# Moving the first half's depthwise convolution wholly to DVE, with the taps split over two running sums

## The chip, the cores and the metric

The kernel runs on one core of one Trainium2 chip. The metric is the device time of one execution in microseconds (us). The engines are named as the profile names them: PE multiplies matrices, DVE is the vector engine, ACT the scalar engine, POOL the small general engine, and SP issues the transfers (DMAs).

## The reference

A two-layer causal trunk over 2048 positions and 1024 channels, in float32. Layer 0 mixes a causal pooling branch with a state-space branch. Layer 1, which the change touches, is a convolution module; `h` is the RMS-normalised input.

```python
proj = einsum('bsd,de->bse', h, w_in)              # 1024 -> 3072
val, gt, z = proj[..., :1024], proj[..., 1024:2048], proj[..., 2048:]
g = val * sigmoid(gt)
# depthwise causal convolution, width 31, one kernel per channel
c = conv(g, conv_w, padding=[(30, 0)]) + conv_b
c = (c - mean(c)) * rsqrt(var(c) + 1e-5) * ln_g + ln_b   # over the channels
y = silu(c) * silu(z)
x = x + einsum('bse,ed->bsd', y, w_out)
```

A final RMS norm follows.

## The kernel before

**Tiles.** The sequence is cut into two halves of 1024 positions, A (h = 0) and B (h = 1), and the channels of layer 1 into eight tiles j = 0 to 7 of 128. Activations lie with channels on the partitions. Every large projection is done in three products, high by high, high by low and low by high parts of the two factors, so a 128-channel output tile over 1024 positions (a unit, such as `A.v3` for the value tile 3 of half A) is 48 matmuls of 512 columns on PE. A unit's sums lie in one of three PSUM buffers `mm`; two smaller PSUM buffers `aux` serve everything else.

**Order on PE.** Layer 0 of A and of B come first, then: A's layer-0 output (`A.glu*`, `A.o.*`), A's layer-1 units (`A.g0` gate, `A.v0` value, and so on, then `A.y0` to `A.y7` for z), B's layer-0 output, B's layer-1 units, A's last projection `A.q.*`, B's last projection `B.q.*`. The table `ORDER` gives the order of the gate and value tiles within a half.

**The convolution.** `post_val` forms the tile g and stores it. Most tiles are convolved on DVE: `conv_load` brings the tile and its 30 positions of history into a buffer `cg`, ACT writes the first tap with the bias into an accumulator `ca`, and `conv_thread` runs the other 30 taps, each `ca = cg[shifted] * weight + ca`, on DVE at the lowest priority. There are two `cg` and two `ca` buffers, so one tile is loaded while the other is summed. The last two tiles of B are done in two passes of 512 positions. The tiles listed in `PEC` are convolved on PE in half B, and those in `PEB` in both halves at once: `pe_conv` builds banded matrices on ACT (24 products of a band with a mask per half tile) and multiplies them in 48 matmuls a tile, whose moving operand has `M = 64 * len(halves)` columns. Before the change DVE has tiles 0 to 5 of A and 0 to 3 of B, and PE has tiles 6 and 7 of both halves together (M = 128) and tiles 4 and 5 of B (M = 64).

**Layer norm.** `ln_thread(h, b)` waits for all eight convolved tiles of a block of 512 positions (b = 0 or 1), loads them into four buffers, and works on DVE and ACT, with three small groups of PE products (mean, variance, spread of the rate) and POOL for the reciprocal root. A's result goes to DRAM (`y1d`) and is loaded again by `y1_thread` when `A.q` is near; B's stays in SBUF.

**What sets the order.** A planner in the kernel (`Sched`) runs at build time. Each piece of work is a thread that yields operations with an assumed duration; the planner picks the operation that can start first, and among those that can start almost as early the one of best priority. The result is one fixed queue for each engine. On the chip each engine runs its queue strictly in that order, and waits where an operand is not there. So a change of the table, of an assumed cost or of the number of buffers moves rows in every queue.

Of the kernel before, what the change touches and what calls it, by code (L numbers as in the profile page):

```python
# [14 lines left out]
AF = mybir.ActivationFunctionType  # L15
ALU = mybir.AluOpType
# [4 lines left out]
H = 1024  # L21
NK = D // 128
# [3 lines left out]
NT = 31  # L26
# [12 lines left out]
SLOTS = dict(act=25, w=8, raw=2, st=8, po=2)  # L39
NSSM = 3  # L40
RANK = dict(split=2, pool=4, pec=3, lna=8, lnb=3, y1=3, ssm=4, prep=2)
PEB = (6, 7)
PEC = (4, 5) + PEB
ORDER = (range(NK), (0, 1, 6, 7, 2, 3, 4, 5))


VECS = {"even_norm": 8, "odd_norm": 8, "pool_scale": 4, "ssm_d": 4, "conv_b": 8, "conv_ln_g": 8, "conv_ln_b": 8}
# [29 lines left out]
class Sched:  # L77
# [24 lines left out]
    def free(self, pool, *tiles):  # L102
        for t in tiles:
            self.pools[pool].append(self.slot.pop(t.tensor.name))

    def done(self, *key):
        self.keys.add(key)

    def spawn(self, gen, prio, name=""):
        self.threads.append(Thread(gen, prio, name))  # L110
# [137 lines left out]
def trunk(ctx, tc, io):  # L248
    nc = tc.nc
    V, A, G, SP = nc.vector, nc.scalar, nc.gpsimd, nc.sync  # L250
    sc = Sched()
    done, free, spawn = sc.done, sc.free, sc.spawn
# [9 lines left out]
    def slots(pool, n, width=1024, where=const):  # L262
        sc.pool(pool, n, lambda i, dt, name: where.tile([128, width], dt, tag=f"{pool}{i}", name=name))
# [4 lines left out]
    slots("st", SLOTS["st"], SLOT)  # L268
    slots("po", SLOTS["po"], SLOT)
    slots("cg", 2, SLOT)  # L270
    slots("ca", 2)
    slots("sml", 12, 16)
    slots("pwt", 1, 128)
    slots("sml2", 1, 64)
# [17 lines left out]
    def width(o):  # L292
        return int(np.prod(o.shape[1:]))
# [20 lines left out]
    def tt(o, a, b, op, eng=None):  # L314
        if eng is G:
            d = 0.35 + 0.2 * width(o) if op == ALU.pow else 0.19 + width(o) * 2e-3
            return Op("G", d, [a, b], [o], lambda: G.tensor_tensor(o, a, b, op))  # L317
        d = vdur(0.16, 1.035e-3, o, a, b)
        return Op("V", d, [a, b], [o], lambda: V.tensor_tensor(o, a, b, op))  # L319
# [14 lines left out]
    def stt(o, a, s, b, op0, op1):  # L334
        rd = [a, b] + ([s] if isinstance(s, bass.AP) else [])
        d = vdur(0.27, 0.935e-3, o, a, b) if isps(a, b) else vdur(0.2, 1.06e-3, o, a, b)
        return Op("V", d, rd, [o], lambda: V.scalar_tensor_tensor(o, a, s, b, op0, op1))  # L337
# [18 lines left out]
    def act(o, a, fn, **kw):  # L356
        rd = [a] + [s for s in kw.values() if isinstance(s, bass.AP)]
        wr = [o]
        if "accum_out" in kw:
            rd.remove(kw["accum_out"])  # L360
            wr.append(kw["accum_out"])
        n = sum(isinstance(s, bass.AP) for s in kw.values())
        return Op("A", adur(o, a, n), rd, wr, lambda: A.activation(o, a, fn, **kw))  # L363
# [24 lines left out]
    def mmb(batch):  # L388

        d = 0.0  # L390
        for o, w, x, s, e in batch:
            if x.dtype == F32R:
                d += width(o) / 2216.0
            elif w.shape[1] > 64:
                d += max(0.224, width(o) * 1e-3)
            else:
                d += 0.07 + width(o) * 0.5e-3

        def emit():
            for o, w, x, s, e in batch:  # L400
                nc.tensor.matmul(o, w, x, start=s, stop=e)  # L401
        rd = []
        wr = []
        for o, w, x, s, e in batch:
            for l, ap in ((rd, w), (rd, x), (wr, o)):
                if not any(ap is y for y in l):
                    l.append(ap)
        op = Op("PE", d, rd, wr, emit)
        op.n = len(batch)
        return op  # L410
# [24 lines left out]
    cwt = ctile("cwt", (128, NK, NT))  # L435
# [16 lines left out]
    def vc(nm, k):  # L452
        return vcol[:, cols[nm] + k:cols[nm] + k + 1]
# [974 lines left out]
    def conv_load():  # L1428
        for h, j in conv_order:
            yield Wait(("g", h, j))  # L1430
            gt = yield Alloc("cg")
            if h == 0:
                yield gset(gt[:, :HL], 0.0)
            else:
                yield dma(gt[:, :HL], gd[0][j][:, H - HL:H])
            yield dma(gt[:, HL:HL + H], gd[h][j])
            cgt[h, j] = gt
            yield Wait(("cw",))
            ca = cas[h, j] = yield Alloc("ca")
            yield act(ca[:, :H], gt[:, 0:H], AF.Identity, bias=vc("conv_b", j), scale=cwt[:, j, 0:1])  # L1440
            done("cg", h, j)

    cgt, cas = {}, {}

    def conv_thread():

        seq = [(h, j, (0, 1)) for h, j in conv_order[:-2]]
        seq += [(h, j, (b,)) for b in range(2) for h, j in conv_order[-2:]]
        for h, j, bl in seq:
            yield Wait(("cg", h, j))  # L1450
            gt, ca = cgt[h, j], cas[h, j]
            n0, n1 = bl[0] * 512, bl[-1] * 512 + 512
            acc = ca[:, n0:n1]
            for k in range(1, NT):
                yield stt(acc, gt[:, k + n0:k + n1], cwt[:, j, k:k + 1], acc, ALU.mult, ALU.add)
            if bl[-1] == 1:
                free("cg", gt)
            spawn(conv_store(h, j, ca, bl), 6, f"cs{h}{j}")

    def conv_store(h, j, ca, bl):  # L1460
        n0, n1 = bl[0] * 512, bl[-1] * 512 + 512
        yield dma(cd[h][j // 2][:, j % 2, n0:n1], ca[:, n0:n1])
        if bl[-1] == 1:
            free("ca", ca)
        for b in bl:
            done("c", h, j, b)
# [15 lines left out]
    def pe_conv(n, j):  # L1482


        halves = (0, 1) if j in PEB else (1,)
        M = 64 * len(halves)
# [51 lines left out]
    def post_val(h, j):  # L1538
        def f(ps):
            yield Wait(("th", h, j))  # L1540
            th = th1.pop((h, j))
            t = th[:, :H]
            if j in PEB or (h == 1 and j in PEC):
                n = PEC.index(j)
# [40 lines left out]
    def ln_thread(h, b, out, gate=None):  # L1585
        if gate:
            yield Wait(gate)
        bs = slice(b * 512, (b + 1) * 512)
        for j in range(NK):
            yield Wait(("c", h, j, b))  # L1590
        if h == 0 or b == 0:
            ct = yield Alloc("act", 4)
            pools = ("act",) * 4
        else:
            pools = ("ca", "ca", "cg", "cg")
            ct = yield Alloc("ca", 2)
            ct += yield Alloc("cg", 2)
        cc = [c[:, :1024] for c in ct]
        for kp in range(4):
            yield dma(k2(cc[kp]), cd[h][kp][:, :, bs])  # L1600
        sm_, vs_, q_ = yield Alloc("st", 3)
        sm, vs, sq = sm_[:, :1024], vs_[:, :1024], q_[:, :1024]
        yield tt(sm, cc[0], cc[1], ALU.add)
        for c in cc[2:]:
            yield tt(sm, sm, c, ALU.add)
        yield tt(sm[:, 0:512], sm[:, 0:512], sm[:, 512:1024], ALU.add)
        mups = yield Alloc("aux")
        yield mmb([(mups, onesN, sm[:, 0:512], True, True)])
        mub = mups.rearrange("p (o t) -> p o t", o=1).to_broadcast([128, 2, 512])
        for kp in range(4):  # L1610
            yield tt(k2(cc[kp]), k2(cc[kp]), mub, ALU.subtract)
        free("aux", mups)
        yield act(vs, cc[0], AF.Square)
        for kp in range(1, 4):
            s = sq if kp % 2 else sm
            yield act(s, cc[kp], AF.Square)
            yield tt(vs, vs, s, ALU.add)
        yield tt(vs[:, 0:512], vs[:, 0:512], vs[:, 512:1024], ALU.add)
        var = yield Alloc("aux")
        yield mmb([(var[:, t:t + 1], vs[:, t * 128:(t + 1) * 128], onesN[:, 0:1], True, True) for t in range(4)])  # L1620
        s = yield Alloc("sml")
        va, rs = s[:, 0:4], s[:, 4:8]
        yield ts(va, var[:, :4], LN_EPS, None, ALU.add)
        free("aux", var)
        yield from rsqrt_of(rs, va, 4)
        dg = sm[:, 0:512]
        for t in range(4):
            yield ts(dg[:, t * 128:(t + 1) * 128], ident, rs[:, t:t + 1])
        rps = yield Alloc("aux")
        yield mmb([(rps[:, t * 128:(t + 1) * 128], ones1, dg[:, t * 128:(t + 1) * 128], True, True) for t in range(4)])  # L1630
        free("sml", s)
        rsb = vs[:, 0:512]
        yield acopy(rsb, rps)
        free("aux", rps)
        free("st", q_, sm_)
        rb = rsb.rearrange("p (o t) -> p o t", o=1).to_broadcast([128, 2, 512])
        for kp in range(4):
            yield tt(k2(cc[kp]), k2(cc[kp]), rb, ALU.mult)
            spawn(ln_out(h, b, kp, cc[kp], out, pools[kp], ct[kp]), 2, f"ln{h}{b}{kp}")
        free("st", vs_)  # L1640
# [102 lines left out]
    y1 = [Acts(f"y1{p}") for p in P]  # L1743
# [107 lines left out]
    spawn(after(("y1d", 0, 3), ln_thread(0, 1, None)), RANK["lna"], "lnA1")  # L1851
    spawn(y1_thread(0, y1[0], ("u", GATE_Y)), RANK["y1"], "y1A0")
    spawn(after((y1[0].name, 7, 0), y1_thread(1, y1[0], ("u", GATE_Y))), RANK["y1"], "y1A1")
    spawn(ln_thread(1, 0, y1[1]), RANK["lnb"], "lnB0")
    spawn(ln_thread(1, 1, y1[1]), RANK["lnb"], "lnB1")
    spawn(fnb_thread(0, ("u", "A.q.e0t3")), 4, "fnb")
    done("fnb", 1)
    sc.run()
# [42 lines left out]
```

## Time and profile before

| | |
|---|---|
| median of 3 runs | 1502.55 us (1501.55 to 1502.56) |
| the profiled execution's own time | 1500.32 us |
| its span, first to last instruction | 1498.5 us, so 1.82 us lie around it |
| PE busy | 98% |
| DVE busy | 74% |
| ACT busy | 35% |
| POOL busy | 6% |
| granted PE clock, mean | 0.995 |
| DMA | 276 MB, 184 GB/s |

The profiled execution is 2.23 us below the median. Sums are made against the profiled execution, and the result is carried over to the median. Times in the text are us from the start of the span. A row of the timeline has the start, the length, the engine, the line of the code, the operation, what it writes and reads, and how many instructions were merged; in square brackets stands the time that the engine sat idle just before it and what ended that.

### The profile page before, as it was taken

The numbers are of one execution on the slowest core, as the hardware profiler recorded it, in microseconds if no ns is written. First come the engines' busy times: TensorE is split into PE (matmuls) and PEld (weight loads), VectorE is DVE, ScalarE is ACT, GpSimd is POOL, SyncE is SP. The second block draws the span as 40 slices with busy tenths as digits, with TensorE's granted clock in tenths as the row PEclk, the third lists the DMA queues.
The fourth block names the chain that finished last, engine by engine and source line by source line (L and its number), as shares of the span: only waits on it lengthen the run. The fifth ranks groups of instructions, "written<-read, shape, count | busy, mean of one in ns | idle before, by whom it ended". The sixth has DMA issues, their size and how long they took to land. (4 is left out here: it accounts for less than half of the span.)

```text
span 1498.5 us, 17919 instructions
## 1 busy us (share of the span) xinstructions
PE 1467.7 (98%) x6768; PEld 1202.1 (80%) x6768; DVE 1104.4 (74%) x1333; ACT 524.7 (35%) x834; POOL 89.7 (6%) x297
## 2 busy tenths in 40 slices
PE   7999899999999999999999999999999999999997
PEld 5887688888888888888888888888888788887785
DVE  7988583997975224699999998247987998987632
ACT  6235341112143035211111521352364556544411
POOL 1000100000000011000000000110000000003321
PEclk9999999999999999999999999999999999999999
DMA  9579946556475462331343543524557475957752
GB/s 350 197 212 335 336 165 247 194 189 239 161 268 151 125 206 85 112 111 59 99 127 113 210 140 128 183 70 128 109 156 227 138 244 185 385 202 248 260 171 109
DMA packets 161159, 276.26 MB, mean 184 GB/s; under 512 B 53184, under 2 KB 83632, under 8 KB 161072
## 3 DMA queue, kind: packets, MB, share of 16 engines
q1 hardware_dynamic: 161072, 275.12, 55.5%
q8 instruction: 53, 0.87, 0.2%
q14 instruction: 34, 0.28, 0.1%
HBM read 181.56 MB, written 93.51 MB: 184 GB/s over the span
## 5 line engine op out<-in xcount | busy, mean ns | idle before, releaser
L401 PE MATMUL mm<-act,w 128*128 128x512 f32 x4224 | 1003.8, 397 | 9.6 <-ACT act L363 6.6
L401 PEld LDWEIGHTS mm<-act,w 128*128 128x128 f32 x4224 | 793.2, 189 | 190.5 <-ACT act L363 6.6
L337 DVE SCALAR_TENSOR_TENSOR ca<-cg,cwt,ca 128x1024 f32<-128x1024 f32 (+1 forms) x360 | 397.5, 1106 | 12.8 <-ACT ca L363 2.5
L401 PE MATMUL mm<-w,act 128*128 128x512 f32 x1344 | 315.9, 395 | 0.8 <-DVE w L319 0.8
L401 PEld LDWEIGHTS mm<-w,act 128*128 128x128 f32 x1344 | 251.7, 188 | 59.4 <-DVE w L319 1.1
L319 DVE TENSOR_TENSOR w<-raw,w 128x1024 fp32r<-128x1024 f32 (+1 forms) x119 | 141.9, 1195 | 106.8 <-ACT w L351 106.1
L351 ACT CAST w<-raw 128x1024 fp32r<-128x1024 f32 (+1 forms) x119 | 121.6, 1022 | 214.9 <-PE mm L401 141.6
L363 ACT ACTIVATE junk<-st 128x1024 bf16<-128x1024 f32 (+1 forms) x64 | 54.0, 844 | 123.8 <-DVE st L319 116.1
L319 DVE TENSOR_TENSOR st<-st,mm 128x512 f32<-128x512 f32 x48 | 30.9, 683 | 76.2 <-PE mm L401 76.2
L351 ACT CAST act<-st 128x512 fp32r<-128x512 f32 (+1 forms) x64 | 51.8, 855 | 57.2 <-DVE st L337 16.6
L363 ACT ACTIVATE po<-mm 128x1024 f32<-128x1024 f32 x28 | 28.7, 1025 | 112.4 <-PE mm L401 70.7
L319 DVE TENSOR_TENSOR act<-st,act 128x512 fp32r<-128x512 f32 (+1 forms) x64 | 56.4, 922 | 14.7 <-ACT act L351 14.6
L401 PE MATMUL aux<-st,act 128*128 128x128 f32 (+2 forms) x448 | 63.8, 289 | 0.0
L363 ACT ACTIVATE act<-act,mask 128x128 f32<-128x128 f32 x192 | 58.0, 392 | 16.5 <-DMA act<-band 16.5
L401 PEld LDWEIGHTS aux<-st,act 128*128 128x128 f32 x448 | 57.2, 191 | 2.9
L363 ACT ACTIVATE st<-mm 128x1024 f32<-128x1024 f32 x24 | 24.6, 1024 | 81.5 <-PE mm L401 81.5
L337 DVE SCALAR_TENSOR_TENSOR act<-aux,vcol,act 128x512 fp32r<-128x512 f32 x32 | 22.6, 746 | 41.0 <-ACT act L363 41.0
L317 POOL TENSOR_TENSOR sml<-sml,mhalf 128x1 f32<-128x1 f32 (+2 forms) x38 | 30.3, 798 | 336.8 <-DVE sml L327 335.2
L351 ACT COPY st<-aux 128x256 f32<-128x256 f32 (+3 forms) x50 | 21.4, 445 | 75.2 <-PE aux L401 56.9
L329 POOL TENSOR_SCALAR sml<-sml 128x1 f32<-128x1 f32 (+2 forms) x72 | 25.7, 357 | 365.3 <-ACT junk L363 360.6
L401 PE MATMUL mm<-act,act 128*128 128x512 f32 x192 | 45.0, 394 | 0.8 <-DVE st L319 0.8
L337 DVE SCALAR_TENSOR_TENSOR st<-st,mm 128x1024 f32<-128x1024 f32 x24 | 34.2, 1424 | 14.7 <-PE mm L401 8.8
(144 smaller groups left out, 873.0 us busy)
## 6 DMA issues: line engine op xcount, KB each, us to landing
raw<-in_odd_w_in SPq DMA_DIRECT2D x48, 512.0 KB, 3.9
st<-x1d SPq DMA_DIRECT2D x48, 256.0 KB, 4.9
raw<-in_even_w_in SPq DMA_DIRECT2D x23, 512.0 KB, 5.7
st<-in_xT SPq DMA_DIRECT2D x16, 512.0 KB, 5.9
st<-in_x SPq DMA_DIRECT2D x16, 512.0 KB, 7.9
raw<-in_even_w_out SPq DMA_DIRECT2D x16, 512.0 KB, 3.9
z1d<-po SPq DMA_DIRECT2D x16, 512.0 KB, 3.2
st<-z1d SPq DMA_DIRECT2D x16, 512.0 KB, 6.5
```

Of the source, the lines that this page charges most:

```text
L317: return Op("G", d, [a, b], [o], lambda: G.tensor_tensor(o, a, b, op))
L319: return Op("V", d, [a, b], [o], lambda: V.tensor_tensor(o, a, b, op))
L329: e.tensor_scalar(o, a, s1, s2, op0, op1)
L337: return Op("V", d, rd, [o], lambda: V.scalar_tensor_tensor(o, a, s, b, op0, op1))
L351: return Op("A", adur(o, a, 0), [a], [o], lambda: A.copy(o, a))
L363: return Op("A", adur(o, a, n), rd, wr, lambda: A.activation(o, a, fn, **kw))
L401: nc.tensor.matmul(o, w, x, start=s, stop=e)
```

## The change

The first half's eight tiles are all convolved on DVE (`PEB` is empty), and PE convolves tiles 4 to 7 of the second half only, all with M = 64. On DVE the even taps go into one accumulator and the odd taps into another; ACT starts both, and DVE adds them at the end. For that there are four `ca` buffers. The layer norm of A takes its four buffers from `ca` and no longer from the general pool `act`, and that of the last block too. The layer norms of B wait until A's result is back in SBUF. Two things change only what the planner assumes or what is free: the cost of a PE product that isn't in the rounded format, and a smaller SBUF reserve for transfers that POOL would issue (the kernel has none; all its transfers are issued by SP).

```diff
-PEB = (6, 7)
-PEC = (4, 5) + PEB
-ORDER = (range(NK), (0, 1, 6, 7, 2, 3, 4, 5))
+PEB = ()
+PEC = (4, 5, 6, 7)
+ORDER = (range(NK), (0, 1, 2, 6, 3, 7, 4, 5))
...
-    slots("ca", 2)
+    slots("ca", 4)
...
             elif w.shape[1] > 64:
-                d += max(0.224, width(o) * 1e-3)
+                d += max(0.224, width(o) * 1.68e-3)
...
-            ca = cas[h, j] = yield Alloc("ca")
+            ca, cb = cas[h, j] = yield Alloc("ca", 2)
             yield act(ca[:, :H], gt[:, 0:H], AF.Identity, bias=vc("conv_b", j), scale=cwt[:, j, 0:1])
+            yield act(cb[:, :H], gt[:, 1:H + 1], AF.Copy, scale=cwt[:, j, 1:2])
...
-            acc = ca[:, n0:n1]
-            for k in range(1, NT):
-                yield stt(acc, gt[:, k + n0:k + n1], cwt[:, j, k:k + 1], acc, ALU.mult, ALU.add)
+            acc = ca[:, n0:n1], cb[:, n0:n1]
+            for k in range(2, NT):
+                yield stt(acc[k % 2], gt[:, k + n0:k + n1], cwt[:, j, k:k + 1], acc[k % 2], ALU.mult, ALU.add)
+            yield tt(acc[0], acc[0], acc[1], ALU.add)
             if bl[-1] == 1:
                 free("cg", gt)
+                free("ca", cb)
...
-        if h == 0 or b == 0:
-            ct = yield Alloc("act", 4)
-            pools = ("act",) * 4
-        else:
-            pools = ("ca", "ca", "cg", "cg")
-            ct = yield Alloc("ca", 2)
-            ct += yield Alloc("cg", 2)
+        pool = "act" if h == 1 and b == 0 else "ca"
+        pools = (pool,) * 4
+        ct = yield Alloc(pool, 4)
...
-    spawn(ln_thread(1, 0, y1[1]), RANK["lnb"], "lnB0")
-    spawn(ln_thread(1, 1, y1[1]), RANK["lnb"], "lnB1")
+    spawn(ln_thread(1, 0, y1[1], (y1[0].name, NK - 1, 1)), RANK["lnb"], "lnB0")
+    spawn(ln_thread(1, 1, y1[1], (y1[0].name, NK - 1, 1)), RANK["lnb"], "lnB1")
...
-    nc = bacc.Bacc("TRN2", target_bir_lowering=False, num_devices=1)
+    nc = bacc.Bacc("TRN2", target_bir_lowering=False, num_devices=1, dynamic_dma_scratch_size=1024)
```

Three places in the queues show what moves. In the rows that follow, `ca` are accumulators, `cg` the convolution's input, `w<-raw` the low part of a weight tile, `st<-st,mm` the evacuation of a unit, and numbers are buffers' names; "x8" is eight such rows in succession.

The first place is DVE's queue while PE does A's gate and value units, around the end of A's first convolution tile. Before:

```order
L337 SCALAR_TENSOR_TENSOR ca_610_4927<-cg_609_4909,cwt,ca_610_4927 128x1024 x8
L319 TENSOR_TENSOR w_643_5351<-raw_635_5240,w_642_5350 128x1024
L337 SCALAR_TENSOR_TENSOR ca_610_4927<-cg_609_4909,cwt,ca_610_4927 128x1024 x5
L337 SCALAR_TENSOR_TENSOR ca_626_5140<-cg_625_5129,cwt,ca_626_5140 128x1024
L337 SCALAR_TENSOR_TENSOR st_641_5349<-st_641_5349,mm_640_5348 128x1024
L319 TENSOR_TENSOR w_648_5415<-raw_639_5302,w_647_5414 128x1024
L337 SCALAR_TENSOR_TENSOR ca_626_5140<-cg_625_5129,cwt,ca_626_5140 128x1024 x8
```

And now:

```order
L337 SCALAR_TENSOR_TENSOR ca_599_4822<-cg_598_4806,cwt,ca_599_4822 128x1024
L337 SCALAR_TENSOR_TENSOR ca_600_4823<-cg_598_4806,cwt,ca_600_4823 128x1024
L337 SCALAR_TENSOR_TENSOR ca_599_4822<-cg_598_4806,cwt,ca_599_4822 128x1024
L319 TENSOR_TENSOR ca_599_4822<-ca_599_4822,ca_600_4823 128x1024
L319 TENSOR_TENSOR w_625_5094<-raw_617_4983,w_624_5093 128x1024
L337 SCALAR_TENSOR_TENSOR ca_611_4929<-cg_610_4911,cwt,ca_611_4929 128x1024
L337 SCALAR_TENSOR_TENSOR ca_612_4930<-cg_610_4911,cwt,ca_612_4930 128x1024
```

Before, one tap follows another into the same accumulator, and only at a tile's end (the rows `x5` and the one behind it) do two neighbours write different ones; now neighbours always do, and a tile ends with an add.

The second place is DVE's queue while PE ends B's layer-0 output (`B.o.e1t2`, `B.o.e1t3`) and transposes its rows for the norm of layer 1. `act<-aux,vcol,act` is the low part of a normalised, transposed tile; it frees the buffer `aux` that PE's next transposes need. Before:

```order
L319 TENSOR_TENSOR st_798_6885<-st_798_6885,mm_797_6884 128x512
L319 TENSOR_TENSOR st_799_6886<-st_799_6886,mm_797_6884 128x512
L337 SCALAR_TENSOR_TENSOR act_812_7025<-aux_813_7026,vcol,act_811_7024 128x512
L337 SCALAR_TENSOR_TENSOR act_812_7025<-aux_814_7037,vcol,act_811_7024 128x512
L319 TENSOR_TENSOR st_805_6964<-st_805_6964,mm_804_6963 128x512
L319 TENSOR_TENSOR st_806_6965<-st_806_6965,mm_804_6963 128x512
L337 SCALAR_TENSOR_TENSOR act_816_7043<-aux_817_7053,vcol,act_815_7042 128x512
L337 SCALAR_TENSOR_TENSOR act_816_7043<-aux_821_7072,vcol,act_815_7042 128x512
L337 SCALAR_TENSOR_TENSOR act_823_7078<-aux_826_7093,vcol,act_822_7077 128x512
L337 SCALAR_TENSOR_TENSOR act_823_7078<-aux_830_7113,vcol,act_822_7077 128x512
```

And now:

```order
L337 SCALAR_TENSOR_TENSOR act_822_7089<-aux_823_7090,vcol,act_821_7088 128x512
L337 SCALAR_TENSOR_TENSOR act_822_7089<-aux_824_7103,vcol,act_821_7088 128x512
L337 SCALAR_TENSOR_TENSOR ca_786_6688<-cg_785_6676,cwt,ca_786_6688 128x1024
L319 TENSOR_TENSOR st_815_7023<-st_815_7023,mm_814_7022 128x512
L319 TENSOR_TENSOR st_816_7024<-st_816_7024,mm_814_7022 128x512
L337 SCALAR_TENSOR_TENSOR act_826_7109<-aux_827_7120,vcol,act_825_7108 128x512
L337 SCALAR_TENSOR_TENSOR act_826_7109<-aux_831_7140,vcol,act_825_7108 128x512
L337 SCALAR_TENSOR_TENSOR ca_787_6689<-cg_785_6676,cwt,ca_787_6689 128x1024
L337 SCALAR_TENSOR_TENSOR ca_786_6688<-cg_785_6676,cwt,ca_786_6688 128x1024
L337 SCALAR_TENSOR_TENSOR act_833_7146<-aux_836_7161,vcol,act_832_7145 128x512
L337 SCALAR_TENSOR_TENSOR act_833_7146<-aux_840_7182,vcol,act_832_7145 128x512
```

A's convolution was over here; now its eighth tile is still running, and one or two taps stand between the pairs of low parts.

The third place is the start of A's first layer norm in DVE's queue. Before, it stands while PE does B's value tile 4 and gate tile 5, between taps of B's last tiles:

```order
L337 SCALAR_TENSOR_TENSOR ca_951_8150<-cg_948_8125,cwt,ca_951_8150 128x512 x13
L319 TENSOR_TENSOR w_978_8408<-raw_959_8243,w_977_8407 128x1024
L337 SCALAR_TENSOR_TENSOR ca_951_8150<-cg_948_8125,cwt,ca_951_8150 128x512 x2
L337 SCALAR_TENSOR_TENSOR ca_968_8364<-cg_967_8344,cwt,ca_968_8364 128x512
L319 TENSOR_TENSOR st_979_8414<-act_971_8384,act_972_8385 128x1024
L319 TENSOR_TENSOR st_979_8414<-st_979_8414,act_973_8386 128x1024
L319 TENSOR_TENSOR st_979_8414<-st_979_8414,act_974_8387 128x1024
```

And now, at B's first gate and value units, right behind the end of A's eighth tile:

```order
L337 SCALAR_TENSOR_TENSOR ca_787_6689<-cg_785_6676,cwt,ca_787_6689 128x1024
L337 SCALAR_TENSOR_TENSOR ca_786_6688<-cg_785_6676,cwt,ca_786_6688 128x1024
L319 TENSOR_TENSOR ca_786_6688<-ca_786_6688,ca_787_6689 128x1024
L319 TENSOR_TENSOR w_881_7482<-raw_857_7295,w_880_7481 128x1024
L337 SCALAR_TENSOR_TENSOR st_879_7480<-st_879_7480,mm_861_7324 128x1024
L319 TENSOR_TENSOR w_891_7526<-raw_860_7319,w_890_7525 128x1024
L319 TENSOR_TENSOR st_887_7519<-ca_882_7489,ca_883_7490 128x1024
L319 TENSOR_TENSOR st_887_7519<-st_887_7519,ca_884_7491 128x1024
L319 TENSOR_TENSOR st_887_7519<-st_887_7519,ca_885_7492 128x1024
```

The norm has moved ahead of all of B's taps, which need the accumulators that it holds. The last add of the eighth tile stands just ahead of the evacuation of B's first value unit (`mm_861`).

More of the change, by code (lines that the diff above doesn't have):

```diff
@@ L1450, in conv_thread @@
             yield Wait(("cg", h, j))
-            gt, ca = cgt[h, j], cas[h, j]
+            gt, (ca, cb) = cgt[h, j], cas[h, j]
             n0, n1 = bl[0] * 512, bl[-1] * 512 + 512
-            acc = ca[:, n0:n1]
-            for k in range(1, NT):
-                yield stt(acc, gt[:, k + n0:k + n1], cwt[:, j, k:k + 1], acc, ALU.mult, ALU.add)
+            acc = ca[:, n0:n1], cb[:, n0:n1]
+            for k in range(2, NT):
+                yield stt(acc[k % 2], gt[:, k + n0:k + n1], cwt[:, j, k:k + 1], acc[k % 2], ALU.mult, ALU.add)
+            yield tt(acc[0], acc[0], acc[1], ALU.add)
             if bl[-1] == 1:
                 free("cg", gt)
+                free("ca", cb)
             spawn(conv_store(h, j, ca, bl), 6, f"cs{h}{j}")
```

## The prediction

> **What bounds the kernel now.** I read the head of the page first: busy times, and PE's and DVE's slices.
>
> ```profile
> PE 1467.7 (98%) x6768; PEld 1202.1 (80%) x6768; DVE 1104.4 (74%) x1333; ACT 524.7 (35%) x834; POOL 89.7 (6%) x297
> PE   7999899999999999999999999999999999999997
> DVE  7988583997975224699999998247987998987632
> ```
>
> PE is busy in every slice but those of the start and the end; DVE is full in long stretches (slices 17 to 24, 27 to 35) and half empty between. PE lacks 30.8 us of the span, so no change elsewhere can gain more than that. Where those lie decides how much this change can reach; next, therefore, PE's timeline, cut to the rows with idle time behind the first 200 us.
>
> ```profile
> 584.62 0.77 PE L415 MATMUL aux<-ident,st 128*128 128x128 f32 x5 [0.17 <-ACT st L363]
> ...
> 991.00 0.76 PE L415 MATMUL aux<-ident,st 128*128 128x128 f32 x5 [0.17 <-ACT st L363]
> 1165.35 1.10 PE L401 MATMUL aux<-st,onesN 128*128 128x512 f32 x2 [0.45 <-DVE st L319]
> 1178.00 1.05 PE L401 MATMUL aux<-onesN,st 128*128 128x1 f32 x8 [0.42 <-DVE st L319]
> 1372.21 1.13 PE L401 MATMUL aux<-st,ones 128*128 128x128 f32 x8 [1.16 <-DVE st L327]
> 1405.08 16.68 PE L401 MATMUL mm<-w,act 128*128 128x512 f32 x71 [0.76 <-DVE w L319]
> 1485.67 3.76 PE L401 MATMUL mm<-act,act 128*128 128x512 f32 x15 [0.78 <-DVE st L319]
> ```
>
> In 1300 us PE waits 3.91 us: 0.34 in the two norms of layer 1, 2.03 in layer norms, 1.54 in the last projections. The remaining 26.9 lie in the start and the end, where the change moves nothing: the first and the last of six idle rows of PE up to 170 us, and the last stretch (us, then PE's busy time).
>
> ```profile
> 6.58 0.79 PE L401 MATMUL mm<-act,w 128*128 128x512 f32 x1 [6.58 <-ACT act L363]
> ...
> 169.28 0.27 PE L415 MATMUL aux<-ident,sml 128*8 128x128 f32 x1 [3.21 <-POOL sml L317]
> ```
>
> ```profile
> 1450.00:1500.00 50.00, 38.65 (x166) 30.73 (x164) 11.57 (x13) 5.79 (x16) 7.43 (x29) 0.92 0.40 137
> ```
> So the time can change in three ways only: PE gets less or more to do, some of the 3.9 us go, or PE meets new waits.
>
> **PE's own work.** The convolution stays 48 matmuls for each of four tiles: before, two with 128 columns and two with 64; now four with 64. The groups by form count these instructions (two for each such matmul), and the timeline shows what they occupy.
>
> ```profile
> L401 PE MATMUL aux<-st,act 128*128 128x128 f32 x192 | 22.6, 275 | 0.0
> L401 PE MATMUL aux<-st,act 128*128 128x64 f32 x192 | 22.2, 273 | 0.0
> ```
>
> ```profile
> 1100.09 2.87 PE L401 MATMUL aux<-st,act 128*128 128x128 f32 x24
> 1102.71 1.62 PE L401 MATMUL mm<-act,w 128*128 128x512 f32 x6
> ...
> 1224.10 2.79 PE L401 MATMUL aux<-st,act 128*128 128x64 f32 x24
> 1226.70 1.64 PE L401 MATMUL mm<-act,w 128*128 128x512 f32 x6
> ```
>
> From a batch's start to that of the next work is 2.62 us at 128 columns and 2.60 at 64. Eight batches change width: 8 x 0.02 = 0.2 us gained. Taking half the products' columns from PE takes nothing from PE that shows.
>
> The Trainium skill, "TensorE: Matmul & The Clock Gate", section "Back-to-back issue gap", lists the isolated gap of a matmul by its moving columns, 134 cycles at 128 and about 60 up to 64. By that rule the 192 instructions would save 74 cycles each, some 5.9 us at 2.4 GHz (an estimate from that page). The two batches above contradict it for this form.
>
> **DVE: the taps.** Two tiles of A come over. What matters is the step from one tap to the next, not its duration.
>
> ```profile
> 661.15 7.76 DVE L337 SCALAR_TENSOR_TENSOR ca<-cg,cwt,ca 128x1024 f32<-128x1024 f32 x6
> 669.16 1.22 DVE L337 SCALAR_TENSOR_TENSOR st<-st,mm 128x1024 f32<-128x1024 f32 x1 [0.25 <-PE mm L401]
> 670.29 1.22 DVE L319 TENSOR_TENSOR w<-raw,w 128x1024 fp32r<-128x1024 f32 x1
> 671.43 10.52 DVE L337 SCALAR_TENSOR_TENSOR ca<-cg,cwt,ca 128x1024 f32<-128x1024 f32 x8
> ...
> 683.30 7.89 DVE L337 SCALAR_TENSOR_TENSOR ca<-cg,cwt,ca 128x1024 f32<-128x1024 f32 x6
> ```
>
> ```profile
> L337 DVE SCALAR_TENSOR_TENSOR ca<-cg,cwt,ca 128x1024 f32<-128x1024 f32 x240 | 307.6, 1284 | 9.3 <-ACT ca L363 2.3
> L337 DVE SCALAR_TENSOR_TENSOR ca<-cg,cwt,ca 128x512 f32<-128x512 f32 x120 | 89.8, 751 | 3.5 <-ACT ca L363 0.2
> ```
>
> Eight taps take 10.52, so one follows another after (10.52 - 1.28) / 7 = 1.32 us: it starts when the one before has ended, since it reads what that one writes. The run of six at 683.30 is of the same kind, 7.89. The run at 661.15 takes 7.76, and by the queue it is the one in which a tile ends: its fifth and sixth tap write different accumulators. This one pair saved 0.13, so a tap that does not need its neighbour follows after 1.19 us. Separate instructions of other kinds do it too: the add-like row at 670.29 lasts 1.22, and the next starts 1.14 after it. With two sums every tap has such a neighbour. A tile costs 29 x 1.19 + 1.14 for the add = 35.7 us, against 30 x 1.32 = 39.6 now.
>
> The Trainium skill, "VectorE: DVE Perf Modes", section "The DRAIN you can't avoid", says that the next Vector operation cannot issue until the pipe is empty. By it the two sums would change nothing in the step; the run of 7.76 against 7.89 speaks against it, and what it would do here is the third rival.
>
> **DVE: does it fit?** The first stretch runs from the first tap to the evacuation of B's first value unit, ahead of which the queue now has the last add of the eighth tile. The window's rows (DVE alone, then the instructions on `ca` alone, where the third busy time is DVE's) and the evacuation before:
>
> ```profile
> 617.90:1014.00 396.10, 326.33 (x281) 1.00 0.38 123
> 1014.00:1242.00 228.00, 198.85 (x199) 1.00 0.60 170
> ```
>
> ```profile
> 617.90:1014.00 396.10, 0.00 (x0) 0.00 (x0) 230.68 (x180) 6.24 (x6) 1.00 0.38 123
> 1014.00:1242.00 228.00, 0.00 (x0) 0.00 (x0) 139.88 (x144) 4.96 (x4) 1.00 0.60 170
> ```
>
> ```profile
> 1014.49 1.22 DVE L337 SCALAR_TENSOR_TENSOR st<-st,mm 128x1024 f32<-128x1024 f32 x1 [2.27 <-PE mm L401]
> ```
>
> Other work is 326.3 - 230.7 = 95.6 us, and eight tiles need 8 x 35.7 = 285.6: 381 of 396 us. It fits, with 15 us to spare. The bound from which DVE is late: a step of (396.1 - 95.6 - 9.1) / 232 = 1.26 us.
>
> The second stretch goes to about 1242, by when PE has done `B.y2` (that is 792 large matmuls at 0.231 us and 16 batches at 2.6 behind 1014) and A's second layer norm follows in the queue. B's four tiles, two in halves of which a tap's step is 0.75 - 0.08 = 0.67: 2 x 35.7 + 4 x (29 x 0.67 + 0.6) = 151.5 us; other work 198.9 - 139.9 = 59. That is 211 of 228. A's first layer norm, with its waits for ACT and POOL, now lies in this stretch with no taps between, since it holds all four accumulators; the 17 us that are left must cover those waits. It is tight, and I take it as enough, because before the two layer norms there cost PE 0.87 us in all.
>
> **The small parts.** ACT copies a second start for each of 12 tiles, nearest row 1.05 us, and starts two tiles more (1.24 each); it loses two of the six re-orderings behind PE's convolution.
>
> ```profile
> L363 ACT ACTIVATE st<-act 128x1024 f32<-128x1024 f32 x12 | 12.2, 1052 | 8.7 <-DVE act L319 5.8 <-DVE st L319 2.7
> L363 ACT ACTIVATE ca<-cg,vcol,cwt 128x1024 f32<-128x1024 f32 x10 | 12.4, 1244 | 39.1 <-DMA cg<-gd 23.5 <-DMA cd<-ca 15.6
> L363 ACT ACTIVATE st<-st,vcol 128x1024 f32<-128x1024 f32 x6 | 12.7, 2124 | 11.2 <-DMA st<-ctd 11.2
> ```
>
> 12.6 + 2.5 - 4.2 = 11 us more, on an engine that is 35% busy: nothing on PE's path, as long as a tile is loaded while the one before is summed, which two `cg` and two pairs of `ca` keep up. POOL has two more fills of `cg`, and they stand in its queue ahead of the roots of B's norm, each waiting for DVE to end a tile; the eighth tile's fill waits for the end of the sixth, 6 x 47 us behind the first tap (a tile each 47: 381 / 8), near 900, and the norm's first root before ran at 948:
>
> ```profile
> 948.07 0.19 POOL L329 TENSOR_SCALAR sml<-sml 128x1 f32<-128x1 f32 x1 [140.88 <-ACT junk L363]
> ```
>
> 48 us of cover; a DVE that is later than that would hold the norm. SP issues as many transfers as before (two `cg` loads and two tile stores more, two pairs of `ctd` fewer). A store waits for its tile with weight fetches queued behind, as now. The smaller reserve, the later gate of B's norms and the planner's cost only move rows: nothing, because PE does not wait for those units now.
>
> **The norm of B.** Here taps now stand in front of rows that free PE's buffers.
>
> ```profile
> 995.06 1.41 DVE L337 SCALAR_TENSOR_TENSOR act<-aux,vcol,act 128x512 fp32r<-128x512 f32 x2 [1.57 <-ACT act L363]
> 998.03 1.41 DVE L337 SCALAR_TENSOR_TENSOR act<-aux,vcol,act 128x512 fp32r<-128x512 f32 x2 [1.55 <-ACT act L363]
> ```
>
> In the second group DVE idles 1.55 us between pairs; one tap of 1.28 fits. In the first group a pair is followed by two taps, or a tap and an evacuation, some 3.8 us with the pair, against 3.7 between PE's transposes. Lower bound: minus 0.2 (today's wait goes). Upper bound: each of the eight pairs is late by a whole tap, 8 x 1.28 = 10 us. I take +0.5, near the lower end, because the excess by rows is 0.1 for each of three or four pairs.
>
> **Sum.** PE's work -0.2, B's norm +0.5, layer norms' waits (0.87 and 1.16 now) unchanged for lack of a reason: 1500.3 + 0.3 in the profiled execution, 1502.8 us carried to the median. A change under 0.2%, 3.0 us, can't be told from none here.
>
> **The rivals.**
> - New waits (slower). The pairs of B's norm, or a layer norm with 17 us of cover in the second stretch, make PE wait by several taps. For it: DVE goes from 82% to 96% of the first stretch. Against it: in slices 17 to 24 DVE is full and PE waits nowhere. Half the upper bound, +5: 1507.5. Chance 0.13. It decides from 3 us, when three of eight pairs miss by a tap.
> - The layer norms' waits go (faster). They now lie where DVE has fewer taps among them. All of 0.87 + 1.16, and the norms' 0.34, give -2.4: 1500.2, which still counts as the same; with the 0.76 too, 1499.4. Chance 0.07, of which I count 0.05 as faster.
> - The taps do not overlap (slower). At 1.32 a tap the first stretch takes 95.6 + 232 x 1.32 + 9.1 = 411, 15 us over; PE waits for that at B's norm and at the first evacuations: 1517. Against it stand five tile ends in the trace, each shorter. Chance 0.05.
> - PE's narrow products are cheaper after all (faster). Cost by columns, half of 2.62 for eight batches, is -10.5: 1492. Chance 0.02.
>
> **How the numbers follow.** No measurable change 0.73, and with the small gains 0.75; slower 0.18; faster 0.07. The range runs from 1499 (all waits near the layer norms gone) to 1508 (half the norm's upper bound); beyond lie the overlap's and the columns' rivals and the worst of the norm's.
>
> **What the changed profile would show.** PE's count stays 6768, with 384 rows of 64 columns and its busy time within 1 us. DVE has 1393 instructions, runs of taps at a step of 1.19, and full slices up to 1010; DVE's eighth tile ends ahead of 1014. PE's idle rows behind 200 us sum to under 7 us. I am wrong if PE waits for DVE's `act` or `st` near 960 to 1010 by more than 3 us, if runs show 1.32, or if a batch of 64 columns takes less among other neighbours.

## The result: 25 us slower, and the profile after

The changed kernel takes 1527.91 us (median of 4 runs, 1525.52 to 1529.52), the kernel before 1502.55 beside it: a ratio of 1.0164, interval 1.0145 to 1.0184. The forecast was 1502.8 us, no measurable change. The profiled execution took 1529.52 us with a span of 1527.5, so 29.0 us more span than before.

The head of the page after, and the slices of PE, DVE and POOL:

```profile
PE 1478.8 (97%) x6768; PEld 1205.5 (79%) x6768; DVE 1148.3 (75%) x1393; ACT 535.1 (35%) x850; POOL 107.1 (7%) x297
PE   7999899999999999999999999989999999999997
DVE  7888583999835123799999999876999986587622
POOL 1000100000000011000000000620000000003221
```

The counts are as forecast, 6768 and 1393. PE is busy for 11 us more with the same instructions, so some of them ran slower; and in POOL's slices there is a new 6 and 2, in an engine whose work is the same 297 instructions. That stands in the slices from 955 to 1031 us, around the norm of B. PE's timeline from 600 us on has most of its idle time there too:

```profile
976.76 0.33 PE L415 MATMUL aux<-ident,st 128*128 128x128 f32 x1 [3.09 <-ACT st L363]
977.80 1.32 PE L415 MATMUL aux<-ident,st 128*128 128x128 f32 x5 [0.71 <-ACT st L363]
1010.15 0.47 PE L415 MATMUL aux<-ident,st 128*128 128x128 f32 x1 [5.17 <-ACT st L363]
1011.19 1.33 PE L415 MATMUL aux<-ident,st 128*128 128x128 f32 x5 [0.57 <-ACT st L363]
1270.66 1.99 PE L401 MATMUL aux<-st,onesN 128*128 128x512 f32 x2 [1.08 <-DVE st L319]
1336.26 1.13 PE L401 MATMUL aux<-st,onesN 128*128 128x512 f32 x2 [1.48 <-DVE st L319]
...
1426.05 24.57 PE L401 MATMUL mm<-w,act 128*128 128x512 f32 x95 [3.51 <-DVE w L319]
```

In the norm PE waits 9.54 us for ACT's `st`, the rows scaled by their rate, and not for DVE. Its granted clock (the last column but two) falls around the waits, as slices of four us show (PE's busy time is the second figure):

```profile
976.00:980.00 4.00, 2.53 (x9) 2.15 (x10) 0.87 (x2) 3.12 (x4) 0.38 (x2) 0.65 0.01 4
1008.00:1012.00 4.00, 1.28 (x5) 0.99 (x6) 0.21 (x1) 2.48 (x3) 1.64 (x7) 0.50 0.00 0
1012.00:1016.00 4.00, 4.00 (x17) 3.31 (x16) 2.70 (x3) 1.08 (x2) 0.00 (x0) 0.66 0.02 4
```

To see where the 29.0 us arise, I took from the two timelines the start of every large matmul, the same in number and order in both, and followed how far the changed kernel lags. The lag grows by these amounts, here with the same for the kernels of the experiments:

| growth of PE's lag behind before, us | after | two sums only | one input | old cost | no gate | roots on ACT | one sum |
|---|---|---|---|---|---|---|---|
| start, to 267 us | 4.2 | 1.6 | 1.1 | 0.0 | 0.9 | 0.9 | 1.6 |
| state-space stage, 267 to 430 | 4.0 | 0.0 | 4.0 | 0.0 | 4.0 | 0.0 | 4.0 |
| norm of B, 957 to 1009 | 13.1 | -0.2 | -0.4 | 14.5 | 13.7 | -0.4 | 13.1 |
| boundary of `A.q` and `B.q`, 1398 to 1410 | 4.9 | 0.7 | 5.9 | 4.8 | -1.3 | -0.5 | 8.4 |
| everything else | 2.9 | -1.4 | 0.9 | 2.0 | 8.2 | 2.0 | 28.3 |
| in all | 29.1 | 0.7 | 11.5 | 21.3 | 25.5 | 2.0 | 55.4 |

The first row is not the change: up to 267 us the queues of all five engines are the same in all these kernels, so it is a difference between executions, and 4.2 of the 29 us are of that kind. Of the norm's 13.1 us, 9.54 are waits. Most of the other 3.6 is PE at the lower clock: busy time times the missing share of the clock gives 2.9 us in the three slices above (an estimate).

Why does ACT scale late? Its rows for the first pair of tiles, before and then after:

```profile
950.66 2.19 ACT L363 ACTIVATE st<-st,sml 128x1024 f32<-128x1024 f32 x2 [1.50 <-POOL sml L317]
```

```profile
965.11 2.19 ACT L363 ACTIVATE st<-st,sml 128x1024 f32<-128x1024 f32 x2 [7.95 <-POOL sml L317]
```

It waits for POOL's roots, 7.95 us in place of 1.50. POOL's timeline of before has such a root in operations of 0.19 us and one power of 0.54:

```profile
948.34 0.54 POOL L317 TENSOR_TENSOR sml<-sml,mhalf 128x1 f32<-128x1 f32 x1
948.96 0.19 POOL L317 TENSOR_TENSOR sml<-sml 128x1 f32<-128x1 f32 x1
949.23 0.19 POOL L317 TENSOR_TENSOR sml<-sml,sml 128x1 f32<-128x1 f32 x1
```

After, the same operations, and then DVE's rows of the same microseconds (the last one reads `mm`, which lies in PSUM):

```profile
956.07 0.57 POOL L329 TENSOR_SCALAR sml<-sml 128x1 f32<-128x1 f32 x1 [46.11 <-ACT junk L363]
956.72 1.46 POOL L317 TENSOR_TENSOR sml<-sml,mhalf 128x1 f32<-128x1 f32 x1
958.26 0.83 POOL L317 TENSOR_TENSOR sml<-sml 128x1 f32<-128x1 f32 x1
959.18 1.11 POOL L317 TENSOR_TENSOR sml<-sml,sml 128x1 f32<-128x1 f32 x1
960.37 2.31 POOL L329 TENSOR_SCALAR sml<-sml 128x1 f32<-128x1 f32 x2
...
964.20 0.87 POOL L317 TENSOR_TENSOR sml<-sml,sml 128x1 f32<-128x1 f32 x1
965.03 0.19 POOL L317 TENSOR_TENSOR sml<-sml 128x1 f32<-128x1 f32 x1
965.30 0.19 POOL L317 TENSOR_TENSOR sml<-sml,sml 128x1 f32<-128x1 f32 x1
```

```profile
955.31 2.47 DVE L337 SCALAR_TENSOR_TENSOR ca<-cg,cwt,ca 128x1024 f32<-128x1024 f32 x2
957.82 1.23 DVE L319 TENSOR_TENSOR ca<-ca,ca 128x1024 f32<-128x1024 f32 x1
958.96 6.06 DVE L337 SCALAR_TENSOR_TENSOR ca<-cg,cwt,ca 128x1024 f32<-128x1024 f32 x5
965.15 1.28 DVE L319 TENSOR_TENSOR st<-st,mm 128x512 f32<-128x512 f32 x2
```

From 958.26 on, POOL's starts lie 0.92, 1.19 and again about 1.2 us apart (two operations in 2.31): beside DVE's taps, which step at 1.19, POOL gets one operation through per tap. At 965.03, when the five taps have ended (958.96 + 6.06), it is back at 0.19. Two roots that took 3.5 us take 10. Here an operation on one column of 128 takes as long a step as the 1024-column instruction beside it.

### The profile page after: what moved, and what is told of

It is laid out like the page before. It is cut to its first block, busy times and chain, and to the rows that moved or that the text cites. A ratio compares the mean times of both kernels' runs of the same rounds, so it can differ in the third digit from the quotient of the medians.

```text
span 1527.5 us, 17997 instructions
## 1 busy us (share of the span) xinstructions
PE 1478.8 (97%) x6768; PEld 1205.5 (79%) x6768; DVE 1148.3 (75%) x1393; ACT 535.1 (35%) x850; POOL 107.1 (7%) x297
## 5 line engine op out<-in xcount | busy, mean ns | idle before, releaser
L337 DVE SCALAR_TENSOR_TENSOR ca<-cg,cwt,ca 128x1024 f32<-128x1024 f32 (+1 forms) x406 | 429.3, 1129 | 1.1 <-ACT ca L363 1.1
L401 PE MATMUL aux<-st,act 128*128 128x64 f32 (+1 forms) x448 | 64.0, 289 | 1.4 <-DVE st L319 1.2
L329 POOL TENSOR_SCALAR sml<-sml 128x1 f32<-128x1 f32 (+2 forms) x72 | 32.0, 446 | 268.6 <-ACT junk L363 264.0
```

Of the source, the lines that this page charges most:

```text
L329: e.tensor_scalar(o, a, s1, s2, op0, op1)
```

## The experiments

**Two sums alone.** The kernel before with the split of the taps, four `ca` buffers and the smaller reserve, and nothing else.

```diff
-            for k in range(1, NT):
-                yield stt(acc, gt[:, k + n0:k + n1], cwt[:, j, k:k + 1], acc, ALU.mult, ALU.add)
+            for k in range(2, NT):
+                yield stt(acc[k % 2], gt[:, k + n0:k + n1], cwt[:, j, k:k + 1], acc[k % 2], ALU.mult, ALU.add)
+            yield tt(acc[0], acc[0], acc[1], ALU.add)
```

> The kernel before with the two running sums alone (four accumulators, the added start on ACT, the add at the end); PE keeps tiles 6 and 7 of both halves, and the planner's cost, the buffers of the layer norms and their gates stay as before. Theory P (POOL is slowed): most of what the changed kernel lost comes from taps of A's convolution beside the roots of B's norm on POOL. Here A's six tiles end some 30 us before that norm, so the roots take 0.2 us each as before, PE waits 0.2 us there, and the time is that of before within 3 us: 1502. Rival S (the two sums themselves, by more ACT starts and denser taps that hold up evacuations): the loss stays, 1510 or more. The step between taps is 1.19 us and an A tile takes 36 us under both.

Measured: 1500.94 us beside 1503.84, ratio 0.9988 (0.9977 to 0.9998), and no growth of the lag above 0.7 us in any row of the table behind the start. DVE's part of the two stretches (third busy time) was 326.33 and 198.85 before, and is now:

```profile
617.90:1014.00 396.10, 395.93 (x1749) 322.75 (x1749) 314.35 (x282) 112.69 (x131) 13.60 (x54) 1.00 0.38 123
1014.00:1242.00 228.00, 227.54 (x1165) 191.57 (x1164) 194.81 (x210) 111.75 (x237) 2.87 (x5) 1.00 0.59 171
```

The two sums free 12.0 us of DVE's busy time in the first stretch, about half of what the prediction's costs for six tiles give (6 x (39.6 - 35.7) = 23.4 us; its 39.6 holds the short idle time behind each dependent tap, which is not busy time). They cost nothing; the loss comes from the rest of the change.

**One input.** The changed kernel, where the 29 taps of A's eighth tile, those that lie in the norm of B, are replaced by reductions that read one tensor of the same size and take about as long. So the kernel leaves out the eighth tile's convolution; its queues keep every row's place.

```diff
+                if (h, j) == (0, 7):
+                    yield red(acc[k % 2][:, 0:64], gt[:, HL:HL + H].rearrange("p (a b) -> p a b", b=16))
+                    continue
                 yield stt(acc[k % 2], gt[:, k + n0:k + n1], cwt[:, j, k:k + 1], acc[k % 2], ALU.mult, ALU.add)
```

> The changed kernel with the 29 taps of A's eighth tile, the one that runs beside B's norm, each replaced by a sum over groups of 16 of one SBUF tile, about as long and at the same places of the queue; the eighth tile's convolution is left out. Theory P: POOL is slowed by Vector instructions with two SBUF inputs, not by a busy DVE. Then POOL's operations of B's norm take 0.2 us as before, PE's 9.5 us of waits there and the 3.7 us lost to the halved clock go, and the time is 13 us below the changed kernel, 1515. Rival Q (DVE's full queue delays the norm's own DVE rows, or any busy DVE slows POOL): the stage keeps its 13 us, 1528.

Measured: 1513.47 us, ratio 1.0072 (1.0055 to 1.0088), 14 us below the changed kernel, and the norm's lag is gone. POOL's second pair of roots, and DVE's reductions beside them:

```profile
964.18 0.19 POOL L329 TENSOR_SCALAR sml<-sml 128x1 f32<-128x1 f32 x1 [5.58 <-ACT junk L366]
964.45 0.54 POOL L317 TENSOR_TENSOR sml<-sml,mhalf 128x1 f32<-128x1 f32 x1
965.07 0.19 POOL L317 TENSOR_TENSOR sml<-sml 128x1 f32<-128x1 f32 x1
```

```profile
963.42 7.97 DVE L340 TENSOR_REDUCE ca<-cg 128x64 f32<-128x1024 f32 x7
```

Seven instructions of DVE in 7.97 us (seven taps took 8.45), and POOL runs as if alone. So it is not that DVE is busy, or that rows stand in front of what PE needs. A reduction also writes less than a tap, 64 columns and not 1024, but other rows rule that out as the cause. At 965.15 in the changed kernel DVE writes 512 columns twice, with one of its two inputs in PSUM, and POOL beside it stays at 0.19 us. In the kernel before, two instructions `ca<-ca,aux` from 1331.72 on write 1024 columns each, again with one input in PSUM, and four operations of POOL beside them take 0.19 to 0.20. What is left is the second tensor that a tap reads from SBUF. The Trainium skill, "SBUF — State Buffer", section "Who interferes with whom", says it: a Vector instruction with two SBUF inputs contends with a GpSimd instruction that reads SBUF, the one that comes second is blocked until the first has ended, and a reduction does not contend on this chip. The rows agree on both, with 1.19 us a step beside taps and 0.27 beside reductions.

**Old cost.** The changed kernel with the planner's assumed cost of an unrounded product put back.

```diff
-                d += max(0.224, width(o) * 1.68e-3)
+                d += max(0.224, width(o) * 1e-3)
```

> The changed kernel with the planner's assumed cost of a PE product outside the rounded format back at 0.001 us a column. In the changed kernel PE gains a lag of 4.2 us between 254 and 430 us, in layer 0's state-space stage, where nothing of the convolution runs. Theory: the new cost reordered that stage, so with the old one PE runs through it as before and the time falls by 4 us, to 1524; B's norm keeps its 13 us. Rival: the lag comes from the smaller reserve or the other buffers, and stays: 1528.

Measured: 1520.81 us, ratio 1.0116 (1.0098 to 1.0134), 7 us below the changed kernel. In the changed kernel PE waits in the state-space stage of layer 0 for DVE at five places, of which the first and the last are

```profile
299.32 0.70 PE L401 MATMUL aux<-st,act 128*128 128x256 f32 x2 [0.45 <-DVE st L319]
...
411.55 0.70 PE L401 MATMUL aux<-st,act 128*128 128x256 f32 x2 [0.47 <-DVE st L319]
```

and with the old cost at none between 250 and 440 us. The five waits are 2.28 us. Most of the rest of the stage's 4.0 is PE busy for longer at a granted clock of 1.00, 164.59 us from 271 to 438 in place of 163.00 from 267 to 430 with the old cost; I have not placed that row by row. The stage lags 4.0 us in each of the four kernels with the new cost and 0.0 in each of the three with the old. Only these 4.0 us are shown to come from the cost. The intervals of the two ratios leave anything from 3 to 11 us for the difference of 7, and in the profiled execution of the changed kernel the other 3 lie in the first 267 us, where the cost moves no row and the other kernels of the table lost 0.0 to 1.6. Whether its other executions lose them there too, I can't tell.

**No gate.** The changed kernel without the new wait of B's layer norms.

```diff
-    spawn(ln_thread(1, 0, y1[1], (y1[0].name, NK - 1, 1)), RANK["lnb"], "lnB0")
-    spawn(ln_thread(1, 1, y1[1], (y1[0].name, NK - 1, 1)), RANK["lnb"], "lnB1")
+    spawn(ln_thread(1, 0, y1[1]), RANK["lnb"], "lnB0")
+    spawn(ln_thread(1, 1, y1[1]), RANK["lnb"], "lnB1")
```

> The changed kernel without the gate that holds B's layer norms until A's result is back. In the changed kernel PE waits 3.5 us at 1426 for a weight tile, whose fetch stands on SP behind the stores of output rows that wait for POOL's roots; with the halved clock behind it this is 4.9 us. Without the gate the fetch stands ahead of those stores. Theory: the 4.9 us go, 1523. Rival: the layer norms of B then compete with A's last layer norm and PE waits there instead: 1528.

Measured: 1528.19 us, ratio 1.0167 (1.0148 to 1.0187): no gain, as the rival had it. The wait of 3.51 us at the boundary of the last projections went, and the layer norms came to wait in its place:

```profile
1350.04 1.31 PE L401 MATMUL aux<-st,onesN 128*128 128x512 f32 x2 [1.93 <-DVE st L319]
1359.23 11.04 PE L401 MATMUL mm<-w,act 128*128 128x512 f32 x46 [1.83 <-DVE act L319]
```

**Roots on ACT.** The kernel with the old cost, and of each single-column root only the power left on POOL; the five small steps around it go to ACT, whose rows for them stay at 0.19 to 0.30 us beside taps.

```diff
         yield tt(o, a, mhalf[:, :n], ALU.pow, G)
+        if n == 1:
+            yield act(tv, o, AF.Square)
+            yield act(tv, tv, AF.Copy, scale=a)
+            yield act(tv, tv, AF.Copy, scale=-0.5, bias=1.5)
+            yield act(o, o, AF.Copy, scale=tv)
...
-        yield ts(ms, ss, 1.0 / D, RMS_EPS, ALU.mult, ALU.add, G)
+        yield act(ms, ss, AF.Copy, scale=1.0 / D, bias=RMS_EPS)
```

> The changed kernel with the planner's cost back at the old value, and with the five small steps around each single-column root (the mean plus epsilon, the square, the two products, the correction) on ACT; only the power itself stays on POOL. The layer norms' four-column roots stay as they are. DVE's queue keeps all its taps before and in the norm of B. Theory P (POOL's operations that read SBUF are held while DVE runs taps with two inputs from SBUF): a root now has one such operation in place of six, so the norm of B, +14.5 us in the run with the old cost, falls to +5 or less, ACT's scale waits under 3 us at each of the three places, and the time is 1506 to 1513. Rival Q (DVE's taps stand in front of what PE needs, and POOL's long operations only go with it): DVE's queue is the same, so the norm still costs 12 us or more and the time stays at 1519 to 1523.

Measured: 1502.17 us beside 1504.11, ratio 0.9986 (0.9973 to 0.9999): below the range that I had given, and all of the loss is gone. POOL's pairs of powers, and DVE's taps beside them, which still stand in front of what PE needs (eight taps and five ahead of the two groups of pairs, where the changed kernel has seven and three):

```profile
949.59 2.11 POOL L317 TENSOR_TENSOR sml<-sml,mhalf 128x1 f32<-128x1 f32 x2 [47.02 <-ACT sml L363]
960.63 2.05 POOL L317 TENSOR_TENSOR sml<-sml,mhalf 128x1 f32<-128x1 f32 x2 [8.93 <-ACT sml L363]
```

```profile
951.22 6.06 DVE L337 SCALAR_TENSOR_TENSOR ca<-cg,cwt,ca 128x1024 f32<-128x1024 f32 x5
...
958.61 9.65 DVE L337 SCALAR_TENSOR_TENSOR ca<-cg,cwt,ca 128x1024 f32<-128x1024 f32 x8
```

The norm as a window, with the old cost alone, and then with the roots on ACT (PE's busy time first, DVE's third, POOL's fifth, then the clock):

```profile
940.00:1035.00 95.00, 85.61 (x382) 69.72 (x381) 72.46 (x71) 35.36 (x48) 30.90 (x48) 0.93 0.38 132
```

```profile
940.00:1035.00 95.00, 95.00 (x445) 77.93 (x444) 84.36 (x83) 48.81 (x94) 7.45 (x8) 1.00 0.45 154
```

DVE does more in the second, 84.36 us of 95, and PE misses nothing. What PE waits for from 600 us on is now 4.62 us, 1.48 and 1.84 in layer norms, 0.52 and 0.78 in the last projections. The wait at the boundary of `A.q` and `B.q` went too. That one is not shown, only argued: a fetch of weights stands on SP behind stores of the result, which wait for DVE, which waits for roots, and in this kernel SP's order there has moved as well. The roots there were long before the change too: a pair took 6.94 us from 1391.20 on before, and 6.62 from 1405.77 on after. What is new at the boundary is the fetch's place: before, one goes out at 1394.33, ahead of the stores at 1397.85; after, it goes out at 1426.03, behind those at 1423.52.

**One sum.** The changed kernel with a single running sum again; the second start on ACT goes too.

```diff
-                yield stt(acc[k % 2], gt[:, k + n0:k + n1], cwt[:, j, k:k + 1], acc[k % 2], ALU.mult, ALU.add)
-            yield tt(acc[0], acc[0], acc[1], ALU.add)
+                yield stt(acc[0], gt[:, k + n0:k + n1], cwt[:, j, k:k + 1], acc[0], ALU.mult, ALU.add)
```

> The changed kernel with one running sum: the tiles' new assignment, order, gate and planner's cost stay, a tap follows its predecessor at 1.32 us again, and the second start on ACT and the last add go. Theory P (the loss comes from POOL's roots beside taps in the norm of B, plus the planner's cost and the last projections, not from how dense the taps are): DVE needs 96 + 232 x 1.32 = 402 us and more for the first stretch of 396, so taps run through the whole norm as well, POOL's operations there take 0.6 to 2 us again, and on top DVE is late for B's first evacuations by 10 us or so: 1530 to 1545. Rival T (the two sums themselves cost, by the tighter use of DVE): one sum is faster than the changed kernel, under 1522.

Measured: 1558.05 us, ratio 1.0359 (1.0334 to 1.0384), 30 us above the changed kernel and worse than expected. The norm costs the same 13.1 us, and POOL's step beside the taps is now 1.33 us:

```profile
956.69 1.24 POOL L317 TENSOR_TENSOR sml<-sml,sml 128x1 f32<-128x1 f32 x1
958.02 2.56 POOL L329 TENSOR_SCALAR sml<-sml 128x1 f32<-128x1 f32 x2
```

It follows DVE's step from 1.19 to 1.32 (seven taps take 9.20 us there, from 952.64 on). The rest arises after 1300 us: the planner has put A's first layer norm behind B's taps, its first products on PE are at 1279.38 in place of 1046.49, and PE waits for A's second. So this run differs from the changed kernel in its order too, and its 30 us are not the price of the step alone.

```profile
1369.78 15.21 PE L401 MATMUL mm<-w,act 128*128 128x512 f32 x54 [16.61 <-ACT act L351]
```

**One tile less on PE.** Two sums alone, and B's tile 4 moved from PE to DVE.

```diff
-PEC = (4, 5) + PEB
+PEC = (5,) + PEB
```

> The kernel before with two running sums (the version of the run two sums only, 1500.9), and tile 4 of the second half moved from PE to DVE: PE convolves tiles 6 and 7 of both halves and tile 5 of the second alone. PE loses four batches of 24 instructions, 4 x 2.60 = 10.4 us by the batches of the trace, whatever their columns. Theory P: DVE has 33 us free from 1014 to 1242 and 11 of 58 behind it, so 30 to 36 us more of taps end the last sum at about 1290 to 1300 in place of 1282, B's layer norms come about 15 us later and cost PE some of the gain: 1490 to 1500. Rival: the layer norms of B are late by the whole of the taps, 30 us, and PE waits for them by more than it saved: over 1505.

Measured: 1511.53 us, ratio 1.0046 (1.0028 to 1.0063), beyond the 1490 to 1500 that I had expected; the rival came true. PE, 1.5 us behind before up to the convolution, was 9.1 us ahead at 1251 us, a gain of 10.6 where four batches are 10.4, and gave it all back in the last 100 us, where B's last sum ends only at 1398 (1282 with two sums alone) and PE waits for the layer norms:

```profile
1447.48 5.89 PE L401 MATMUL mm<-w,act 128*128 128x512 f32 x12 [3.73 <-ACT act L351]
1456.12 0.72 PE L401 MATMUL mm<-w,act 128*128 128x512 f32 x2 [2.75 <-ACT act L351]
```

The best of all are two sums alone (0.9988) and roots on ACT (0.9986), which these runs do not tell apart; both are 0.1% below the kernel before, less than the 0.2% that I count as measurable.

## Why the prediction was wrong, step by step

**PE's work: right.** All 384 instructions of the convolution have 64 columns and take as long as before:

```profile
L401 PE MATMUL aux<-st,act 128*128 128x64 f32 x384 | 44.4, 273 | 0.0
```

That is 44.4 us against 22.6 + 22.2. The rival by columns is out. PE's busy time was to stay within 1 us and grew by 11. That is the same instructions at a lower clock for the most part: by the mean clocks, 0.995 and 0.989, about 9 us (an estimate), and 1.6 in the state-space stage at a clock of 1.00.

**The taps' step: right.** Five in 6.06 and seven in 8.45 us give 1.195 a step; 1.19 was forecast. The rival that taps do not overlap is out.

**DVE fits: right.** I had 381 us of 396 in the first stretch and 211 of 228 in the second. In the kernel with the roots on ACT, where no lag shifts the windows, DVE's third busy time is

```profile
617.90:1014.00 396.10, 396.10 (x1751) 323.22 (x1750) 383.45 (x341) 123.91 (x177) 8.19 (x14) 1.00 0.38 129
1014.00:1242.00 228.00, 228.00 (x1172) 192.32 (x1170) 207.90 (x231) 115.28 (x262) 1.81 (x5) 1.00 0.49 152
```

and PE is busy in all of both. The eighth tile's sum ends at 1009.7 there. The cover of POOL's last fill of `cg`, 48 us, measured 46.11 (POOL's idle time ahead of 956.07).

**"The norm of B", +0.5 us: this is the step that failed.** It measured 13.1 in place of 0.5, beyond the upper bound of 10, because the bound counted the wrong thing. I weighed what taps in DVE's queue do to DVE's rows, and of POOL only where its fills stand, and took the length of its roots as unchanged by what runs beside them. The run with the roots on ACT shows that DVE's queue was harmless: with as many taps or more in front of the pairs the norm costs nothing. POOL's queue has eight operations up to the end of the first root, two of the second root's among them; at DVE's step of 1.19 that is 9.5 us, and it took 9.0 (964.20 + 0.87 - 956.07), so that ACT waited 6.45 us more than before. The profile of before had the sign. Late in the norm of B, one power takes 1.52 us and not 0.54, and DVE begins an instruction with two SBUF inputs just then:

```profile
987.05 1.52 POOL L317 TENSOR_TENSOR sml<-sml,mhalf 128x1 f32<-128x1 f32 x1
```

```profile
986.94 1.23 DVE L319 TENSOR_TENSOR w<-raw,w 128x1024 fp32r<-128x1024 f32 x1 [1.60 <-ACT w L351]
```

The group of these powers showed it as well, with a mean of 0.689 us where the shortest takes 0.54:

```profile
L317 POOL TENSOR_TENSOR sml<-sml,mhalf 128x1 f32<-128x1 f32 x32 | 22.0, 689 | 1.4
```

I read POOL's first row of the norm, 0.19 us long and beside an idle DVE, and did not ask for the spread within the group.

**"Only move rows: nothing", for reserve, gate and planner's cost: failed for the cost.** It is worth 4.0 us in the state-space stage, in every kernel of the table that has it, and I had considered its effect only around the convolution. Taking the gate out gained nothing, and the reserve cost nothing (two sums alone has it). The wait of 3.51 us at the boundary of the last projections was in none of my terms. PE's idle rows behind 200 us, which were to sum to under 7 us, sum to 19.6.

**"Layer norms' waits unchanged": near.** They were 2.03 us, and are 1.08 + 1.48 after and 1.48 + 1.84 in the run with roots on ACT.

**The rivals.** "New waits" had the right side, with a fifth of the size and the wrong engine: in the norm PE waits for ACT, and ACT for POOL, and no row of it names DVE. "The layer norms' waits go" did not come: there are fewer, but longer.

Put together: moving the roots' small steps is worth 1.0116 - 0.9986 = 1.3%, 19.5 us. In the table that is 14.9 in the norm, which is shown to be POOL held by DVE, and 5.3 at the boundary, where the cause is argued, less 0.9 at the start. The planner's cost is shown for 4.0 us of the 7 between the medians. Without both, the rest of the change gives 1502.2 beside 1504.1, near what was forecast for the whole.

## What to carry to other kernels

When work is moved onto an engine, look at what its neighbours do in the same microseconds, not only at its own queue: in these traces a small operation of POOL on the path between two engines cost up to a whole DVE instruction, a step of 1.2 us in place of 0.27, where DVE read two tensors from SBUF. Look for it in the groups of before: a mean well above the shortest row of the same shape, as 0.689 above 0.54 here, can say that the operation is already being held somewhere. And a constant of a planner is part of the change in every stage that it prices.

## What the runs showed of the hardware that I had not expected

- POOL beside DVE with two SBUF inputs: operations of 128x1 that start 0.27 us apart alone start 1.19 us apart beside taps with that step and 1.33 beside taps of 1.32; beside reductions with one input they stay at 0.27, and beside DVE instructions with one of two inputs in PSUM they stay at 0.19 us long.
- A wait can cost PE more than its length. Around 5.17 us of waiting the granted clock was 0.50 from 1008 to 1012 us and 0.66 in the four after; around 3.09 us it was 0.65 for four. The length alone does not tell: around the wait of 1.08 us it was 0.67 from 1269 to 1274, and around the one of 1.48 us it stayed at 1.00 from 1336 to 1341.
